# Two-layer trunk on one core: held modulation sums, solved rows on ScalarE, rope work kept out of the lead-in

## Chip, core and metric

One core of a Trainium2 chip runs the whole program. It has a matrix engine (TensorE, PE in the profile, with its weight loads as PEld), a vector engine (VectorE, DVE), a scalar engine (ScalarE, ACT), a general one (GpSimd, POOL) and an engine that issues the DMAs (SyncE, SP). Each engine takes its own instructions strictly in order; between engines they wait on semaphores. The metric is the device time of one launch in microseconds, the median of several runs.

## The reference

A decoder trunk of two layers on one sequence of 1024 tokens, 1024 wide, all in float32. Every layer norms its input, shifts and scales it with modulation vectors, projects it once, runs three token mixers on parts of the projection (causal pooling, retention with rotary positions, RWKV-7), gates and merges their outputs and adds the result back. Cut to what matters here:

```python
def rwkv7_time_mix(p, ...):
    ...
    def step(S, inp):
        r_t, w_t, k_t, v_t, a_t, b_t = inp
        sa = jnp.einsum('bhvk,bhk->bhv', S, a_t)
        S = (S * w_t[:, :, None, :] + sa[..., None] * b_t[:, :, None, :]
             + v_t[..., None] * k_t[:, :, None, :])
        return S, jnp.einsum('bhvk,bhk->bhv', S, r_t)
    _, y = lax.scan(step, jnp.zeros((B, H, N, N), jnp.float32), xs)
    ...

def rotary(x, positions):
    ang = positions.astype(jnp.float32)[..., None] * freqs
    cos, sin = jnp.cos(ang)[:, :, None, :], jnp.sin(ang)[:, :, None, :]
    ...

def hybrid_layer(x, c_act, positions, ...):
    mod = c_act @ w_ada + b_ada
    shift, scale, gate = jnp.split(mod[:, None, :], 3, axis=-1)
    h = rms_norm(x, norm_g) * (1.0 + scale) + shift
    proj = h @ w_in
    ...
    y = jnp.einsum('btnw,nwd->btnd', branches, w_branch)
    gates = jax.nn.sigmoid(gate_logits.reshape(B, T, N_BRANCHES, D))
    return x + gate * (jnp.sum(gates * y, axis=2) @ w_out)

def reference(x, c, positions, ...):
    c_act = jax.nn.silu(c)
    for l in range(2):
        x = hybrid_layer(x, c_act, positions, ...)
    return rms_norm(x, final_g)
```

## The kernel before

**Tiles.** The activations lie with channels on the 128 partitions and tokens in the free dimension, in two halves of 512 tokens; a 1024-wide tensor is 8 such tiles per half (kt 0 to 7). Float32 products are made of three passes: each operand is split into a rounded high part and the remainder (`hhi`/`hlo` for activations, `wh`/`wl` for weights), and high x high, low x high and high x low are summed in PSUM (`acc`). The high part is a cast, usually on ScalarE; the remainder is a subtraction on VectorE or GpSimd.

**The plan.** The Python program does not issue its instructions as it runs. From the lead-in on, each call is logged as an `Op` on one of five engines (`Log.call`, L217), so that all rows of the profile carry the helper's line, L540. `Log.plan` (L334) then lists them: at each point the engine that can start first takes the operation with the lowest key among those that are ready, by planned costs. The key is the place in the program plus a bias of the lane (`BIAS`): scan operations (lane rwkv) are put 3000 places ahead, modulation sums (lane ada) 1500 behind. Operations marked as free may go to VectorE or GpSimd, whichever the plan finds free. An entry `o.after[p] = 2` holds o until the planned start of p; it orders the plan and makes no semaphore. `emit` (L537) issues the result, and each engine keeps that order.

**Lead-in** (`lead_in`, L1810). The first three projections run while the norm and the modulation are still made. The modulation of layer 0 comes in groups: group g's weights are multiplied by the conditioning vector and added up on VectorE (`ada`, L696: eight rows, `ada_ps`, the last of them `ada_acc`), TensorE sums over the partitions (`sums`, one column each), and two small rows on VectorE make `mod` and `acoef` (`ada_end`, L736). With these ScalarE makes a tile's `hhi`, and a second activation makes the same value in full in place (`affine`, L1770); a subtraction (`low`, L1778) gives `hlo`; nine matmuls use both (`mms`, L1798). `coef(g)` is the whole of group g; groups 4 and 5 serve kt 4 to 7, and the call `coef(5)` ends the last of them. After the lead-in `setup_rest` (L661) loads and scales further vectors (`bone`, `vec`, `omu`), and `rope_tables` (L757) makes the sines and cosines for the two halves: `posi` and `ang`, some ten rows of range reduction on VectorE (`nrot`, `over`), two sines on ScalarE, and DMAs to DRAM (`rope_d`), from which `cs` tiles are read later.

**The scan** (`rwkv_task`, L1285). RWKV-7 runs as 16 chunks for each of 4 pairs of heads in each of 2 layers: 128 steps. In each, ScalarE scales the state (`SP`), TensorE multiplies the state (`two`), VectorE adds (`xst`), TensorE solves the chunk with a prepared inverse (`ch<-xst,G`), the solved rows are copied out of PSUM into `Z` (L1538), TensorE makes the state's update (`ch<-Z,BKt`), VectorE adds it to `S` (two rows), and TensorE makes the outputs (`two<-Z,G`), which ScalarE copies (`y`). Between these TensorE fills its time with the layer's large projections.

**Behind the scan** come the gate projections, merged by seven-product forms (sums of operands `T`, `wsum` on VectorE, then the same splitting), and the output projection. The other ten modulation groups, two of layer 0 and eight of layer 1 (`late_ada`, L1912), are queued in lane ada at this place of the program; a group is loaded in 256 KB tiles (`wada`), added up in `ada_acc` and summed by TensorE into `adaps`. They have no hold, so the plan starts them wherever VectorE has room, from inside layer 0's last scan on.

Of the kernel before, what the change touches and what calls it, by code (L numbers as in the profile page):

```python
# [12 lines left out]
AF = mybir.ActivationFunctionType  # L13
ALU = mybir.AluOpType
# [3 lines left out]
P = 128  # L18
# [186 lines left out]
class Log:  # L205


    def __init__(self, nc, tc):
        self.nc, self.tc = nc, tc
        self.on = False  # L210
        self.ops = []
        self.tag = {}
        self.acc = {}
        self.lane = ""
        self.group = None
        self.real = {"DVE": nc.vector, "POOL": nc.gpsimd}
        self.vector = Proxy(self, "DVE", nc.vector)  # L217
        self.scalar = Proxy(self, "ACT", nc.scalar)
        self.gpsimd = Proxy(self, "POOL", nc.gpsimd)
        self.tensor = Proxy(self, "PE", nc.tensor)  # L220
        self.sync = Proxy(self, "SP", nc.sync)

    def call(self, eng, name, real, a, k):
# [7 lines left out]
        if isinstance(o, Op):  # L231
            o.calls.append((real, a, k, name))
            o.outs += outs
            o.ins_ += ins
        else:
            o = Op()
            o.eng, o.calls, o.outs, o.ins_ = eng, [(real, a, k, name)], list(outs), list(ins)
            o.lane, o.n, o.late, o.inst = self.lane, name, not self.on, None
            o.no_dep = o.own_dep = o.behind = None
            o.held = False  # L240
            o.flex = self.on and FLEX and eng == "POOL" and name == "tensor_tensor" and self.lane in FREE and k.get("op") != ALU.pow
            o.after, o.allocs, o.took = {}, [], []
            o.idx = len(self.ops)
            self.ops.append(o)
            if self.on and self.group is not None:
                self.group = o
# [307 lines left out]
def trunk_kernel(ctx, tc, xT, cvec, pos, vecs, consts, w_ada, w_all, pool_w, lora_w, out):  # L554
# [374 lines left out]
    def add(k, task):  # L929
        if not lanes[k]:  # L930
            due[k] = clock[0]
        lanes[k].append(task)
        return task
# [351 lines left out]
    def rwkv_task(l, hp, kT, rT, vp, lt, lw):  # L1285
# [228 lines left out]
        for c in range(16):  # L1514
# [18 lines left out]
            for hd in range(2):  # L1533
# [1 line left out]
                u0 = (16 * hd + c) * P  # L1535
                n = min(65, 32 * P - u0 - 64)
                mmul(ch[0:n, cols], Gf[:, u0 + 64 : u0 + 64 + n], xst[:, cols])
            nc.vector.tensor_copy(Z[0:64, c, :], ch[0:64, 0:P])  # L1538
            yield wait(Z)
            mmul(ch[:, P : 2 * P], BKt[:, c, :], Z[:, c, :])  # L1540
            for hd in range(2):
# [228 lines left out]
    def affine(h, kt):  # L1770
        x = xin[h][kt]
        b, a = mod[0][:, SHIFT[kt] : SHIFT[kt] + 1], acoef[0][:, kt : kt + 1]
        hi, lo = hb("hhi"), hb("hlo")
        nc.scalar.activation(hi, x, AF.Identity, bias=b, scale=a)
        nc.scalar.activation(x, x, AF.Identity, bias=b, scale=a)
        h_cur[h].append((hi, lo))

    def low(eng, h, kt):  # L1778
# [27 lines left out]
    def steps(g, n):  # L1806
        for _ in range(n):
            next(g)

    def lead_in():  # L1810
        V, G_ = nc.vector, nc.gpsimd
# [30 lines left out]
        def coef(g):  # L1842
            if g in COLUMNS:
                ada_columns(g)
            else:
                steps(gs[g], 9)

        def one(h, kt):
            normed(h, kt)
            affine(h, kt)  # L1850
            low(G_, h, kt)
            mms(h, kt)
# [33 lines left out]
        one(1, 3)  # L1886
        one(0, 5)
        coef(5)
        one(1, 4)
        one(0, 6)  # L1890
        one(1, 5)
# [15 lines left out]
    for i in range(3):  # L1907
        evac(FIRST[i], acc6[1][i], 1)
    wprep()
    setup_rest()  # L1910
    add("mix", rope_tables())
    late_ada = [(0, g) for g in (6, 7)] + [(1, g) for g in range(8)]  # L1912

    for l in range(L):
# [46 lines left out]
                evac(it, ps, h)  # L1961
        assert not lanes["rwkv"] and not lanes["mix"]
        gate_ada = []
        add("ada", iter([30000]))
        while late_ada:
            task = add("ada", ada(*late_ada.pop(0), t_lt))
            if len(gate_ada) < 2:
                gate_ada.append(task)
        TT = [[] for _ in range(4)]
# [413 lines left out]
```

## Time and profile before

| | us |
|---|---|
| three runs | 2290.06, 2287.49, 2287.57 |
| median | 2287.57 |
| the profiled execution, its own time | 2284.81 |
| its span in the profile | 2282.9 |
| TensorE busy | 2246.9 |
| VectorE busy | 1627.5 |
| ScalarE busy | 907.4 |
| GpSimd busy | 623.8 |

The profiled execution's time is the span and 1.9 us around it. The mean granted clock of TensorE is 0.996. Matmuls overlap: one of 512 columns is shown with 0.39 us, but the next starts 0.227 us after it, so starts, not durations, tell the pace. "128x512 x6" stands for six like instructions in a run, and the number in brackets at a row's end is the idle time ahead of it, with the instruction that ended it. Stages in the trace: the lead-in up to about 115 us, layer 0's scan up to about 690, its gates and output up to about 1200, then layer 1.

### The profile page before, as it was taken

The numbers are of one execution on the slowest core, as the hardware profiler recorded it, in microseconds if no ns is written. First come the engines' busy times: TensorE is split into PE (matmuls) and PEld (weight loads), VectorE is DVE, ScalarE is ACT, GpSimd is POOL, SyncE is SP. The second block draws the span as 40 slices with busy tenths as digits, with TensorE's granted clock in tenths as the row PEclk, the third lists the DMA queues.
The fourth block names the chain that finished last, engine by engine and source line by source line (L and its number), as shares of the span: only waits on it lengthen the run. The fifth ranks groups of instructions, "written<-read, shape, count | busy, mean of one in ns | idle before, by whom it ended". The sixth has DMA issues, their size and how long they took to land.

```text
span 2282.9 us, 35125 instructions
## 1 busy us (share of the span) xinstructions
PE 2246.9 (98%) x13076; PEld 1866.6 (82%) x13076; DVE 1627.5 (71%) x2907; ACT 907.4 (40%) x1671; POOL 623.8 (27%) x545
## 2 busy tenths in 40 slices
PE   7999999999999999999999999999999999999998
PEld 6788888888888888888888888888888888888888
DVE  7997876878888644667677778688785844465854
ACT  5734433434235344323454344243332444442243
POOL 2223323323325201331122232332432500041211
PEclk9999999999999999999999999999999999999999
DMA  8212111112356633664541111111122633256442
GB/s 317 81 49 67 33 44 47 44 50 76 117 165 210 213 126 97 226 191 164 170 131 34 41 33 39 56 39 47 51 71 75 194 116 111 88 171 225 133 131 84
DMA packets 138043, 248.86 MB, mean 109 GB/s; under 512 B 15632, under 2 KB 18960, under 8 KB 137872
## 3 DMA queue, kind: packets, MB, share of 16 engines
q1 hardware_dynamic: 137872, 246.61, 33.9%
q8 instruction: 103, 1.69, 0.3%
q14 instruction: 68, 0.56, 0.1%
HBM read 187.04 MB, written 59.51 MB: 108 GB/s over the span
## 4 chain that ended last, share of the span: by engine, by line
PE 89%; DVE 8%; issue 1%; ACT 1%; DMA 0%; POOL 0%; SPq 0%; DVEq 0%; POOLq 0%; ACTq 0%
PE acc L540 73%; PE two L540 3%; PE ch L540 3%; PE av L540 1%; PE ro L540 1%; PE g L540 1%; DVE two L540 1%; DVE tm L540 1%; DVE ksq L540 1%; PE lw L540 1%; PE m L540 1%; PE rkv L540 1%; PE bt L540 1%; DVE G L540 1%; PE rs L540 0%
## 5 line engine op out<-in xcount | busy, mean ns | idle before, releaser
L540 PE MATMUL acc<-hhi,wh 128*128 128x512 f32 x1488 | 599.3, 403 | 0.6 <-DVE vp L540 0.6
L540 PE MATMUL acc<-hlo,wh 128*128 128x512 f32 x1488 | 598.5, 402 | 0.0
L540 PE MATMUL acc<-hhi,wl 128*128 128x512 f32 x1488 | 595.9, 401 | 0.0
L540 POOL TENSOR_TENSOR wl<-wr,wh 128x512 fp32r<-128x512 f32 x175 | 237.9, 1361 | 582.2 <-ACT wh L540 485.3
L540 PEld LDWEIGHTS acc<-hhi,wh 128*128 128x128 f32 x1488 | 280.6, 189 | 51.2 <-issue 1.5
L540 PEld LDWEIGHTS acc<-hhi,wl 128*128 128x128 f32 x1488 | 280.7, 189 | 49.2 <-issue 0.7
L540 PEld LDWEIGHTS acc<-hlo,wh 128*128 128x128 f32 x1488 | 280.8, 189 | 48.6 <-issue 0.7
L540 ACT CAST wh<-wr 128x512 fp32r<-128x512 f32 x242 | 149.1, 617 | 292.8 <-PE acc L540 230.0
L540 PE MATMUL acc<-T,wh 128*128 128x512 f32 x576 | 177.5, 390 | 0.0
L540 PEld LDWEIGHTS acc<-T,wh 128*128 128x128 f32 x576 | 108.2, 188 | 22.4
L540 DVE TENSOR_TENSOR wl<-wsum,wh 128x512 fp32r<-128x512 f32 x75 | 53.5, 713 | 94.8 <-ACT wh L540 94.4
L540 ACT COPY y<-two 64x128 f32<-64x128 f32 x128 | 32.9, 257 | 211.7 <-PE two L540 208.2
L540 PE MATMUL acc<-T,wl 128*128 128x512 f32 x288 | 112.3, 390 | 0.0
L540 DVE SCALAR_TENSOR_TENSOR S<-ch,pc,SP 64x64 f32<-64x64 f32 x256 | 71.9, 281 | 54.8 <-PE ch L540 46.8
L540 POOL TENSOR_TENSOR oz<-ol,oz 128x512 fp32r<-128x512 f32 x10 | 14.3, 1435 | 327.9 <-DVE wl L540 259.2
L540 ACT CAST wh<-wsum 128x512 fp32r<-128x512 f32 x96 | 59.5, 620 | 95.8 <-PE acc L540 93.7
L540 DVE TENSOR_TENSOR xst<-two,MT 64x128 f32<-64x128 f32 x128 | 37.5, 293 | 68.9 <-PE two L540 44.9
L540 DVE TENSOR_TENSOR two<-two,tm 64x30 f32<-64x30 f32 (+14 forms) x240 | 78.8, 328 | 7.0
L540 DVE TENSOR_TENSOR tm<-MT,two 64x30 f32<-64x30 f32 (+14 forms) x240 | 76.3, 318 | 8.2 <-ACT two L540 1.3
L540 DVE TENSOR_TENSOR wl<-wraw,wh 128x512 fp32r<-128x512 f32 x53 | 37.6, 710 | 61.5 <-ACT wh L540 61.5
L540 PE MATMUL acc<-oy,wh 128*128 128x512 f32 x256 | 80.0, 394 | 0.0
L540 PE MATMUL acc<-oG,wh 128*128 128x512 f32 x256 | 79.0, 390 | 0.0
(328 smaller groups left out, 4899.6 us busy)
## 6 DMA issues: line engine op xcount, KB each, us to landing
wr<-in_w_all SPq DMA_DIRECT2D x268, 256.0 KB, 2.7
wraw<-in_w_all SPq DMA_DIRECT2D x96, 256.0 KB, 2.7
gd<-gsg SPq DMA_DIRECT2D x96, 256.0 KB, 2.0
gs<-gd SPq DMA_DIRECT2D x96, 256.0 KB, 3.8
wada<-in_w_ada SPq DMA_DIRECT2D x80, 256.0 KB, 3.1
ol<-od SPq DMA_DIRECT2D x48, 256.0 KB, 3.4
traw<-hd SPq DMA_DIRECT2D x32, 256.0 KB, 3.0
x<-in_xT SPq DMA_DIRECT2D x16, 256.0 KB, 5.1
```

What stands on the lines that cost most here:

```text
L540: o.inst = f(*a, **k)
```

## The change

Four edits; the amount of work stays as it is.

1. `Z`, the copy of the solved rows, goes from VectorE to ScalarE (128 rows).
2. In `affine` the second activation goes to VectorE for kt 6 and 7 (four rows).
3. What `setup_rest` and `rope_tables` put on VectorE, ScalarE and GpSimd is not planned ahead of the start of `coef(5)`'s last operation. Their DMAs have no hold.
4. What the ten late modulation groups put on these three engines is not planned ahead of the start of the last scan operation of layer 0. Their DMAs and matmuls have no hold of their own.

```diff
@@ Log.call
+            if self.quiet is not None and eng in ("DVE", "ACT", "POOL"):
+                o.after[self.quiet] = 2
@@ rwkv_task
-            nc.vector.tensor_copy(Z[0:64, c, :], ch[0:64, 0:P])
+            nc.scalar.copy(Z[0:64, c, :], ch[0:64, 0:P])
@@ affine
-        nc.scalar.activation(x, x, AF.Identity, bias=b, scale=a)
+        if kt < 6:
+            nc.scalar.activation(x, x, AF.Identity, bias=b, scale=a)
+        else:
+            nc.vector.tensor_scalar(x, x, a, b, op0=ALU.mult, op1=ALU.add)
@@ 
+    coefs = []
+
+    def quietly(gen, until_=None):
+        while True:
+            nc.quiet = until_ or coefs[0]
+            dt = next(gen, None)
+            nc.quiet = None
+            if dt is None:
+                return
+            yield dt
@@ lead_in
         coef(5)
+        coefs.append(nc.ops[-1])
@@ 
+    nc.quiet = coefs[0]
     setup_rest()
-    add("mix", rope_tables())
+    nc.quiet = None
+    add("mix", quietly(rope_tables()))
@@ for l in range(L)
+        last_ = next(o for o in reversed(nc.ops) if o.lane == "rwkv")
...
-            task = add("ada", ada(*late_ada.pop(0), t_lt))
+            task = add("ada", quietly(ada(*late_ada.pop(0), t_lt), last_))
```

The plan moves other rows too. Three places, each as it was and as it is now (the helper's line is L543 in the changed kernel).

VectorE in the lead-in, around the sums of group 4 (`ada_acc_204`) and the start of group 5 (`ada_ps_213`); before:

```order
L540 TENSOR_SCALAR vec_101<-vec_101 128x28
L540 SCALAR_TENSOR_TENSOR ada_ps_205<-ringG_130,fixed,ada_ps_205 128x512
L540 TENSOR_SCALAR vec_101<-vec_101 128x4 x2
L540 SCALAR_TENSOR_TENSOR ada_ps_205<-ringG_130,fixed,ada_ps_205 128x512 x2
L540 SCALAR_TENSOR_TENSOR ada_acc_204<-ringG_130,fixed,ada_ps_205 128x512
L540 CAST ang_280<-posi_279 128x512
L540 TENSOR_SCALAR ada_ps_213<-wada_189,fixed 128x512
L540 TENSOR_TENSOR wl_230<-wr_231,wh_229 128x512
L540 SCALAR_TENSOR_TENSOR ada_ps_213<-wada_189,fixed,ada_ps_213 128x512
L540 TENSOR_TENSOR mod_108<-sums_157,vec_100 128x4
L540 SCALAR_TENSOR_TENSOR ada_ps_213<-wada_189,fixed,ada_ps_213 128x512
L540 SCALAR_TENSOR_TENSOR acoef_110<-mod_108,vec_100 128x2
```

and in the changed kernel:

```order
L543 TENSOR_TENSOR wbig_139<-wr_188,wbig_139 128x512
L543 SCALAR_TENSOR_TENSOR ada_ps_205<-ringG_130,fixed,ada_ps_205 128x512 x5
L543 SCALAR_TENSOR_TENSOR ada_acc_204<-ringG_130,fixed,ada_ps_205 128x512
L543 TENSOR_SCALAR ada_ps_213<-wada_189,fixed 128x512
L543 SCALAR_TENSOR_TENSOR ada_ps_213<-wada_189,fixed,ada_ps_213 128x512 x2
L543 TENSOR_TENSOR mod_108<-sums_157,vec_100 128x4
L543 SCALAR_TENSOR_TENSOR acoef_110<-mod_108,vec_100 128x2
L543 SCALAR_TENSOR_TENSOR ada_ps_213<-wada_189,fixed,ada_ps_213 128x512
L543 SCALAR_TENSOR_TENSOR ada_ps_213<-wada_190,fixed,ada_ps_213 128x512
```

The rows of `vec`, `ang` and the weight remainder `wl_230` are gone from this stretch (`bone` and `omu`, a little ahead of it, as well), and `mod` and `acoef` follow each other behind three rows of group 5; before, two of these stood ahead of `mod` and one behind it. The remainders `wl_230` and `wbig_137` are made on GpSimd now.

ScalarE at the sines of the second half, early in the first scan (`y` ends one step, `SP` begins the next); before:

```order
L540 ACT_TABLE_LOAD
L540 ACTIVATE nrot_294<-nrot_294 64x512
L540 ACTIVATE nrot_294<-ang_293 64x512
L540 COPY y_417<-two 64x128
L540 CAST wh_384<-wr_386 128x512
L540 COPY pu_408<-acc_402 128x512
L540 ACTIVATE SP_424<-S_406,pc_270 128x128
L540 CAST pw_436<-pwraw_438 128x128
L540 COPY y_417<-two 64x128
L540 ACTIVATE SP_441<-S_405,pc_270 128x128
L540 CAST pdh_446<-pd_444 128x512
L540 CAST wh_387<-wr_389 128x512
```

and in the changed kernel:

```order
L543 ACTIVATE SP_443<-S_406,pc_270 128x128
L543 ACT_TABLE_LOAD
L543 ACTIVATE nrot_294<-nrot_294 64x512
L543 COPY Z_269<-ch_445 64x128
L543 ACTIVATE nrot_294<-ang_293 64x512
L543 CAST pdh_446<-pd_444 128x512
L543 COPY y_417<-two 64x128
L543 ACTIVATE SP_448<-S_405,pc_270 128x128
L543 ACT_TABLE_LOAD
L543 ACTIVATE silu_428<-acc_416 128x512
L543 CAST wh_395<-wr_397 128x512
L543 COPY Z_269<-ch_449 64x128
```

`Z` stands between `SP` and `y` in every step. The second half's sines (`nrot_294`) have moved three steps on, and both `Z` here have a table load between their step's `SP` and them.

VectorE at the end of layer 0's last scan (`xst`, `Z` and `S` are the scan's, `T` and `traw` belong to the forms behind it); before:

```order
L540 TENSOR_TENSOR traw_1285<-traw_1285,traw_1286 128x512
L540 COPY Z_1032<-ch_1264 64x128
L540 SCALAR_TENSOR_TENSOR rob_1243<-rot_1242,vec_100,silu_1179 128x512
L540 SCALAR_TENSOR_TENSOR ada_acc_1460<-wada_1477,fixed,ada_acc_1460 128x256
L540 SCALAR_TENSOR_TENSOR S_1195<-ch_1264,pc_1033,SP_1263 64x64 x2
L540 SCALAR_TENSOR_TENSOR ada_acc_1460<-wada_1477,fixed,ada_acc_1460 128x256
L540 TENSOR_SCALAR ada_acc_1497<-wada_1498,fixed 128x256
L540 TENSOR_TENSOR xst<-two,MT_1117 64x128
L540 SCALAR_TENSOR_TENSOR ada_acc_1497<-wada_1498,fixed,ada_acc_1497 128x256
L540 SCALAR_TENSOR_TENSOR ada_acc_1497<-wada_1499,fixed,ada_acc_1497 128x256
L540 TENSOR_TENSOR mod_109<-adaps_1496,vec_101 128x2
L540 COPY Z_1032<-ch_1266 64x128
```

and in the changed kernel:

```order
L543 TENSOR_TENSOR traw_1286<-traw_1286,traw_1283 128x512
L543 SCALAR_TENSOR_TENSOR S_1195<-ch_1264,pc_1029,SP_1263 64x64 x2
L543 TENSOR_TENSOR yc_1234<-yc_1234,vr_1236 128x512
L543 TENSOR_TENSOR xst<-two,MT_1117 64x128
L543 TENSOR_TENSOR traw_1285<-traw_1285,traw_1286 128x512
L543 SCALAR_TENSOR_TENSOR rob_1249<-rot_1248,vec_100,silu_1179 128x512
L543 TENSOR_TENSOR wl_1169<-wr_1170,wh_1168 128x512
L543 SCALAR_TENSOR_TENSOR S_1194<-ch_1266,pc_1029,SP_1265 64x64 x2
L543 TENSOR_REDUCE mn_1267<-y_1246 128x8
L543 TENSOR_SCALAR mn_1267<-mn_1267 128x8
L543 TENSOR_TENSOR T_1302<-traw_1275,T_1302 128x512
L543 TENSOR_TENSOR T_1303<-traw_1283,T_1303 128x512
```

The modulation rows (`ada_acc`, `mod`) that lay between the scan's rows are gone from here, and the rows of `Z` with them.

More of the change, by code (lines that the diff above doesn't have):

```diff
@@ L215, in __init__ @@
         self.group = None
+        self.quiet = None
         self.real = {"DVE": nc.vector, "POOL": nc.gpsimd}
```

## The prediction

> **What bounds the kernel now.** I read the page first (busy time, then the chain of waits), after it the list of what TensorE waited for, and then the timeline at the places of the three edits.
>
> ```profile
> PE 2246.9 (98%) x13076; PEld 1866.6 (82%) x13076; DVE 1627.5 (71%) x2907; ACT 907.4 (40%) x1671; POOL 623.8 (27%) x545
> PE 89%; DVE 8%; issue 1%; ACT 1%; DMA 0%; POOL 0%; SPq 0%; DVEq 0%; POOLq 0%; ACTq 0%
> ```
>
> TensorE is busy for 2246.9 of 2282.9 us, and the chain that ended last runs through it. The change leaves all its matmuls in place, so only the 36 us in which it stands idle, and matmuls that ran slower than others of their kind, can be won. VectorE at 71% and ScalarE at 40% matter where TensorE waits for them:
>
> ```profile
> PE sums L540 <- DVE sq L540: 6.8, 2, 6.1
> PE acc L540 <- ACT hhi L540: 3.1, 3, 2.2
> PE ch L540 <- DVE Z L540: 2.7, 4, 1.2
> PE acc L540 <- DVE hlo L540: 0.9, 1, 0.9
> PE adaps L540 <- DVE ada_acc L540: 0.7, 2, 0.5
> PE acc L540 <- DVE vp L540: 0.6, 1, 0.6
> ```
>
> The columns are us in total, times, and the longest. The largest wait, for sq, lies at the program's start, which no edit touches. The waits for hhi, hlo and vp belong to the lead-in, those for Z to the scan, those for ada_acc to the modulation sums: these the edits can reach, some 8 us in all.
>
> **The lead-in.** TensorE sums modulation group 4, then stands still until the first operand that needs the result is there:
>
> ```profile
> 52.83 0.95 PE L540 MATMUL sums<-fixed,ada_acc 128*128 128x1 f32 x8
> 56.01 2.92 PE L540 MATMUL acc<-hhi,wbig 128*128 128x512 f32 x6 [2.23 <-ACT hhi L540]
> 58.73 1.00 PE L540 MATMUL acc<-hlo,wbig 128*128 128x512 f32 x3
> ...
> 47.63 0.68 DVE L540 TENSOR_SCALAR vec<-vec 128x28 f32<-128x28 f32 x1
> 51.10 0.75 DVE L540 SCALAR_TENSOR_TENSOR ada_acc<-ringG,fixed,ada_ps 128x512 f32<-128x512 f32 x1
> 51.77 0.42 DVE L540 CAST ang<-posi 128x512 f32<-128x512 int32 x1
> 52.89 0.69 DVE L540 TENSOR_TENSOR wl<-wr,wh 128x512 fp32r<-128x512 f32 x1
> 54.16 0.15 DVE L540 TENSOR_TENSOR mod<-sums,vec 128x4 f32<-128x4 f32 x1
> 54.95 0.15 DVE L540 SCALAR_TENSOR_TENSOR acoef<-mod,vec 128x2 f32<-128x2 f32 x1
> 55.14 0.81 ACT L540 ACTIVATE hhi<-x,mod,acoef 128x512 fp32r<-128x512 f32 x1 [2.28 <-DVE acoef L540]
> ```
>
> The sums end at 53.78 (52.83 + 0.95). mod starts at 54.16 because VectorE is still at a piece of group 5, and another such piece stands between mod and acoef (54.95 - 54.16 = 0.79 between their starts, though mod takes 0.15). VectorE got behind by work that nobody needs yet: the vector scaling, the rope cast, one weight remainder. In the new order these rows stand behind group 5's coefficients, mod and acoef stand side by side, and three pieces of group 5 are done before the sums end. So mod starts at about 53.8, acoef 0.13 later, hhi 0.19 behind that (55.14 - 54.95): at 54.14 instead of 55.14. I take 0.95 us, and TensorE's gap shrinks from 2.23 to about 1.3. Less than nothing can't come of it, since ScalarE had 2.28 us idle ahead of hhi; the other bound is 0, if the weight remainder that goes to GpSimd in this order, or a row that I don't see, is late in VectorE's stead.
>
> The length of the gap matters twice:
>
> ```profile
> 56.00:58.00 2.00, 1.99 (x5) 1.61 (x6) 1.97 (x4) 1.97 (x3) 0.00 (x0) 0.50 0.17 67
> 59.00:60.00 1.00, 1.00 (x5) 0.81 (x5) 0.96 (x3) 1.00 (x3) 0.72 (x1) 0.97 0.68 262
> 1131.00:1135.00 4.00, 2.28 (x11) 1.50 (x10) 3.90 (x7) 2.08 (x4) 3.51 (x2) 1.00 0.54 205
> ...
> 29.82 1.44 PE L540 MATMUL sums<-fixed,sq 128*128 128x1 f32 x6 [2.04 <-DVE mod L540]
> 30.00:34.00 4.00, 4.00 (x14) 3.52 (x15) 3.28 (x7) 1.76 (x3) 1.28 (x1) 0.50 1.07 390
> ...
> 1133.93 0.50 PE L540 MATMUL acc<-mhi,wl 128*128 128x512 f32 x1 [1.72 <-POOL wl L540]
> ...
> 817.56 293.05 PE acc L540 x1288
> ```
>
> The third number from the right is the granted clock. It is 0.50 behind the gap of 2.23 us and behind an earlier one of 2.04, but 1.00 around a gap of 1.72. The nine matmuls behind the longer gap take from 56.01 to 59.73 (58.73 + 1.00), 3.7 us. The last row, of the chain of waits, has the pace at full clock: 293.05 / 1288 = 0.227 us each, so nine are 2.0. The clock costs 1.7 at most; I take 1.5, as the end of the last matmul overlaps with its successor. A gap of 1.3 lies below the 1.72 that cost nothing, so I count the 1.5 as won, with 0 as the other bound.
>
> [...]
>
> Two more stalls in the lead-in go with the edit of the x affine and the rope rows:
>
> ```profile
> 74.08 1.28 ACT L540 ACT_TABLE_LOAD   x1
> 75.38 0.63 ACT L540 ACTIVATE lt<-lt 64x512 f32<-64x512 f32 x1
> 75.92 0.80 ACT L540 ACTIVATE x<-x,mod,acoef 128x512 f32<-128x512 f32 x1
> 76.75 0.69 DVE L540 TENSOR_TENSOR hlo<-x,hhi 128x512 fp32r<-128x512 f32 x1 [1.35 <-ACT x L540]
> 77.49 0.50 PE L540 MATMUL acc<-hlo,wbig 128*128 128x512 f32 x1 [0.95 <-DVE hlo L540]
> ```
>
> The last x sits on ScalarE behind a table load; VectorE waits for it 1.35 us and TensorE 0.95 (1.1 with the pipeline's refill). With x on VectorE the pair x, hlo needs two rows of about 0.7 there and doesn't wait for ScalarE; in the new order it stands right behind the small vector work (some 1.9 us), far ahead of 77. That is 1.1 won. The wait for vp (0.6) was behind rope rows on VectorE; those are now later than the second evacuation, so I count it as won, 0 as the bound. The four x rows cost VectorE 4 x 0.7 = 2.8 us in a stretch in which it loses the rows above; if that cover fails, one hlo is late by 0.7. The rope's results come later with them: in the new order the second half's sine falls three scan steps later, and its first reader on VectorE stands four steps behind it, so I let nothing wait. Lead-in: 0.95 + 1.5 + 1.1 + 0.6 = 4.2 us won, bounds 1.7 (only the last two) and 4.5.
>
> **Z on ScalarE.** The scan has 128 steps, each with one Z. An ordinary step, the one bad step, and the copy's price on the new engine:
>
> ```profile
> 360.13 0.28 DVE L540 COPY Z<-ch 64x128 f32<-64x128 f32 x1 [0.76 <-PE ch L540]
> 360.91 0.38 PE L540 MATMUL ch<-Z,BKt 128*128 128x128 f32 x2
> ...
> 1721.44 1.75 DVE L540 SCALAR_TENSOR_TENSOR pd<-pt,pu 128x512 f32<-128x512 f32 x1 [0.82 <-POOL pt L540]
> 1723.22 0.28 DVE L540 COPY Z<-ch 64x128 f32<-64x128 f32 x1
> 1723.55 0.49 PE L540 MATMUL ch<-Z,BKt 128*128 128x128 f32 x2 [1.19 <-DVE Z L540]
> ...
> L540 ACT COPY y<-two 64x128 f32<-64x128 f32 x128 | 32.9, 257 | 211.7 <-PE two L540 208.2
> L540 ACT CAST wh<-wr 128x512 fp32r<-128x512 f32 x242 | 149.1, 617 | 292.8 <-PE acc L540 230.0
> ```
>
> In the ordinary step Z is done at 360.41 and used at 360.91: 0.5 us to spare. A copy of that shape out of PSUM takes 257 ns on ScalarE (the y row) against 280, so the copy itself is worth nothing. What counts is the queue ahead of it. On VectorE that was once a row of 1.75 us, twice modulation rows of the last scan; these waits, 2.7 in all, are the whole gain, and I take 2.4. On ScalarE I counted in the new order what stands between a step's SP and its Z: nothing in 46 steps, one of 512 columns (or small ones) in 57, two in 13, and more in four; the remaining eight are first steps, whose SP comes early. SP is done some 1.4 us before Z can start, so one or two rows of 0.6 fit. Of the four, two have a table load (1.28) ahead of Z: 1.28 + 0.6 to 1.28 + 1.2 is late by 0.5 to 1.1 once 1.4 is taken off, and two of 1.8 and 2.4 by 0.4 to 1.0, each less the 0.5 to spare. I take 1.0 lost, bounds 0 and 2.5. VectorE has 128 x 0.28 = 36 us less to do, which shows nowhere else, since TensorE waits for it at no other place of the scan for over 0.7.
>
> [...] In this trace the next activation starts 0.02 us behind the load (74.08 + 1.28 = 75.36, then 75.38). [...]
>
> **The held sums.** The first answer is that of the modulation rows alone in the last scan, the others are all engines behind it:
>
> ```profile
> 500.00:690.00 190.00, 3.19 (x24) 3.27 (x24) 23.46 (x35) 1.00 0.38 116
> ...
> 690.00:725.00 35.00, 35.00 (x157) 28.96 (x157) 29.77 (x36) 18.89 (x35) 23.82 (x17) 1.00 0.68 220
> 725.00:760.00 35.00, 35.00 (x159) 29.04 (x159) 26.42 (x40) 14.20 (x25) 10.39 (x8) 1.00 0.60 195
> ```
>
> 23.46 us of VectorE in 35 rows move behind the scan's end at about 690, with 24 one-column matmuls (the DMAs aren't held, so their queue keeps its order nearly). VectorE has 5.2 and 8.6 us free in the two stretches there, TensorE none: what the sums push back there, TensorE feels. But the sums rank lowest in the plan, and in the new order only one of their rows stands among the first 25 behind the scan, ahead of which all first operands of the forms are made. Nothing reads them before the layer's end. The price is that of their own matmuls' waits: 0.7 in two waits for six groups before, so 0.6 more for four more groups; bounds 0 and 9.7 (23.46 less 13.8 free), the latter as a rival.
>
> **Sum.** -4.2 - 2.4 + 1.0 + 0.6 = -5.0 us. The profiled execution took 2284.81 us for a span of 2282.9, so it would be 2279.8; it stands 2.8 below the median of the runs, 2287.57, and the runs are what counts: 2282.6. A plan that is drawn up anew shifts other rows too; from the size of the small waits above (0.6 to 1.7 each) I allow 3 us either way.
>
> **Rivals.**
>
> 1. The clock halves again behind the shorter gap. For it: 2.04 us were enough, and nothing says where between 1.72 and 2.04 it turns, or that length alone decides. The 1.5 is gone: 2284.1.
>
> 2. The gap in the lead-in stays, since something else is late (the weight remainder on GpSimd, the sums themselves): the edit doesn't do what it says. Against it: 2.28 us of ScalarE's idle time end with acoef. 0.95 + 1.5 are gone and one of the small stalls returns: 2286.
>
> 3. Z is late on ScalarE, and the kernel is slower. Place: every step in which a 617 ns cast starts just before Z can. To spare are 0.5 us in good steps and less in others, and a cast that in turn waits for TensorE (230 of the 292.8 us idle ahead of casts ended with acc) drags Z along, as a copy has to wait for what is ahead in its queue. Such a step loses about 0.3. It decides from 5 / 0.3, some 17 steps, on. If it strikes the half of the steps with a row ahead, 64 x 0.3 = 19 us are lost, less what is won: about 2297 for some 50. Against it: the plan keeps Z ahead of casts (46 steps with nothing), and ScalarE is busy only 40% of the time.
>
> 4. The held sums crowd VectorE behind the scan: 9.7 us of operands late in 690 to 760, 2282.6 - 0.6 + 9.7 = 2291.7. It decides when sums stand ahead of the forms' operands; the order speaks against it.
>
> 5. The new plan packs better elsewhere with 36 us less on VectorE: 3 us more, 2279.6.
>
> **How the numbers follow.** Forecast 0.48 (its own range 2279.5 to 2285.5), rival 1 0.14, rival 2 0.08, rival 3 0.14, rival 4 0.08, rival 5 0.08. A measurement of this kernel tells about 0.2% (4.6 us) from no change, so faster is below 2283.0 and slower above 2292.1. Faster: three quarters of the forecast, 0.36, all of rival 5, a little of rival 1: 0.46. Slower: nearly all of rival 3, half of rival 4: 0.18. Same: 0.36. The range for 8 in 10 goes from 2277, where the upper bounds of the gains and the better plan lie, to 2292, which takes in rivals 1, 2 and most of 4, and leaves out rival 3.
>
> **What would show it.** In the profile after: TensorE's wait for hhi at about 55 is near 1.3 and the clock of the next 2 us is 1.00 (step one right; 0.50 is rival 1); no wait for hlo at 75 and none for vp near 93; the line "ch <- Z" names ACT with about 1 us in two to five waits (20 or more waits are rival 3); in 690 to 760 TensorE stays fully busy (if not, rival 4). The prediction is wrong if TensorE's idle time is not about 5 us less, or if the idle time is less and the span isn't, as matmuls then ran slower than I take them to.

## The result, and the profile after

The changed kernel takes 2278.0 us (median of 5 runs, 2277.56 to 2279.91) against 2287.57 (5 runs, 2285.1 to 2290.06): a ratio of 0.9960 with a 95% interval of 0.9948 to 0.9971, so 6.6 to 11.9 us less. The forecast was 5.0 us less. The profiled execution is the median one, 2278.0, and its span 2275.7 us, 7.2 shorter than the span before; the medians differ by 9.6, since the profiled execution before was 2.8 below its median. TensorE's idle time in the spans went from 36.0 to 28.5 us.

What TensorE waited for in the changed kernel, in the list that the prediction began with (us in total, times, longest):

```profile
PE acc L543 <- ACT hhi L543: 1.8, 2, 1.3
PE acc L543 <- POOL wl L543: 1.7, 1, 1.7
PE two L543 <- DVE S L543: 1.2, 4, 0.4
PE nps L543 <- ACT sg L543: 1.2, 2, 0.8
PE adaps L543 <- DVE ada_acc L543: 0.5, 1, 0.5
PE ch L543 <- ACT Z L543: 0.2, 1, 0.2
```

The waits for hlo and vp are gone, the longest for hhi is at 1.3 instead of 2.2, that for Z at 0.2 instead of 2.7. New are small waits for S and for sg. The lead-in, TensorE first, then VectorE and ScalarE:

```profile
52.83 0.95 PE L543 MATMUL sums<-fixed,ada_acc 128*128 128x1 f32 x8
55.07 2.19 PE L543 MATMUL acc<-hhi,wbig 128*128 128x512 f32 x6 [1.30 <-ACT hhi L543]
57.06 1.49 PE L543 MATMUL acc<-hlo,wbig 128*128 128x512 f32 x3
58.34 1.81 PE L543 MATMUL acc<-hhi,wbig 128*128 128x512 f32 x5
...
53.81 0.16 DVE L543 TENSOR_TENSOR mod<-sums,vec 128x4 f32<-128x4 f32 x1
54.01 0.16 DVE L543 SCALAR_TENSOR_TENSOR acoef<-mod,vec 128x2 f32<-128x2 f32 x1
...
54.20 0.81 ACT L543 ACTIVATE hhi<-x,mod,acoef 128x512 fp32r<-128x512 f32 x1 [3.24 <-DVE acoef L543]
```

The sums end where they ended before, at 53.78. mod follows at 53.81, acoef at 54.01, hhi at 54.20, and TensorE stands still for 1.30 us: as worked out. But look at the rows behind the gap: nine matmuls from 55.07 to 58.34 take 3.27 us, where nine at full clock, 0.227 us each, take 2.0. In the windows of the same profile (the third number from the right is the granted clock):

```profile
54.00:56.00 2.00, 0.93 (x4) 0.80 (x5) 1.69 (x4) 1.76 (x3) 0.00 (x0) 0.99 0.22 85
56.00:58.00 2.00, 2.00 (x7) 1.51 (x6) 1.81 (x3) 1.97 (x3) 0.00 (x0) 0.50 0.35 131
58.00:60.00 2.00, 2.00 (x8) 1.59 (x7) 1.55 (x3) 2.00 (x4) 0.39 (x1) 0.65 0.34 131
```

The clock is whole until 56 and halved then, a little later than before. So the first rival came true at this place, and yet the kernel gained more than the forecast. The rest must come from the scans.

**A wait that the list doesn't show.** Here is a step of layer 1's scan before, VectorE and then TensorE. The list of waits has no wait for Z in this step, since no row carries a bracket:

```profile
1459.92 0.68 DVE L540 TENSOR_TENSOR rot<-acc,cs 64x512 f32<-64x512 f32 x1
1460.64 0.28 DVE L540 COPY Z<-ch 64x128 f32<-64x128 f32 x1
...
1459.41 0.40 PE L540 MATMUL ch<-xst,G 128*65 128x64 f32 x4
...
1460.52 0.47 PE L540 MATMUL acc<-hhi,wh 128*128 128x512 f32 x1
1460.98 0.49 PE L540 MATMUL ch<-Z,BKt 128*128 128x128 f32 x2
```

The solved product is done at 1459.81. VectorE began a row of rot at 1459.92, and Z had to wait until 1460.64. It ended at 1460.92, and TensorE's product of it started 0.06 behind. The matmul ahead had started at 1460.52, so the next could have begun 0.23 later, at 1460.75: 0.23 us were lost. The list calls TensorE idle only from the shown end of a matmul, 0.47 behind its start, and so misses some 0.2 us of each wait of this kind. By starts, a step is late when `ch<-Z` begins within 0.08 us of Z's end, and what it loses is the distance from the matmul ahead beyond 0.23. Before, that is 10 steps with 2.9 us in layer 0 and 8 with 2.4 in layer 1: 5.3 us where the list had 2.7 in four waits. In all 18, Z stands directly behind a row of VectorE (rot seven times, also ksq, ka, wl, traw and others, of 0.16 to 1.75 us). So it does in 68 of the other 110 steps too; the 18 have in common that Z starts 0.69 us or more behind the solved product, where the median of the others is 0.04. In the changed kernel one step of the 128 is late, by 0.4 us.

### The profile page after: what moved, and what is told of

Its sections match the earlier page's. It is cut to its first block, busy times and chain, and to the rows that moved or that the text cites. A ratio compares the mean times of both kernels' runs of the same rounds, so it can differ in the third digit from the quotient of the medians.

```text
span 2275.7 us, 35073 instructions
## 1 busy us (share of the span) xinstructions
PE 2247.2 (99%) x13076; PEld 1868.3 (82%) x13076; DVE 1613.4 (71%) x2779; ACT 934.2 (41%) x1795; POOL 626.1 (28%) x549
## 4 chain that ended last, share of the span: by engine, by line
PE 90%; DVE 6%; issue 1%; ACT 1%; DMA 1%; POOL 0%; SPq 0%; DVEq 0%; POOLq 0%; ACTq 0%
PE acc L543 74%; PE two L543 3%; PE ch L543 2%; PE g L543 1%; PE av L543 1%; PE ro L543 1%; DVE ksq L543 1%; PE m L543 1%; PE bt L543 1%; PE lw L543 1%; PE rkv L543 1%; PE rs L543 1%; DVE G L543 0%; PE pps L543 0%; DVE two L543 0%
## 5 line engine op out<-in xcount | busy, mean ns | idle before, releaser
L543 PE MATMUL acc<-hhi,wh 128*128 128x512 f32 x1488 | 597.9, 402 | 0.0
L543 PE MATMUL acc<-hhi,wl 128*128 128x512 f32 x1488 | 596.9, 401 | 0.0
L543 PE MATMUL acc<-hlo,wh 128*128 128x512 f32 x1488 | 596.3, 401 | 0.0
L543 POOL TENSOR_TENSOR wl<-wr,wh 128x512 fp32r<-128x512 f32 x164 | 222.6, 1359 | 563.0 <-ACT wh L543 402.5
L543 PEld LDWEIGHTS acc<-hhi,wh 128*128 128x128 f32 x1488 | 280.5, 189 | 49.8 <-issue 1.8
L543 PEld LDWEIGHTS acc<-hhi,wl 128*128 128x128 f32 x1488 | 280.4, 188 | 49.6 <-issue 0.7
L543 PEld LDWEIGHTS acc<-hlo,wh 128*128 128x128 f32 x1488 | 280.5, 189 | 49.4 <-issue 1.1
L543 ACT CAST wh<-wr 128x512 fp32r<-128x512 f32 x242 | 149.1, 617 | 264.7 <-PE acc L543 202.6
L543 PE MATMUL acc<-T,wh 128*128 128x512 f32 x576 | 178.1, 390 | 0.0
L543 DVE SCALAR_TENSOR_TENSOR S<-ch,pc,SP 64x64 f32<-64x64 f32 x256 | 72.2, 282 | 87.0 <-PE ch L543 83.9
L543 PEld LDWEIGHTS acc<-T,wh 128*128 128x128 f32 x576 | 108.0, 188 | 22.3
L543 PE MATMUL acc<-T,wl 128*128 128x512 f32 x288 | 112.4, 390 | 0.0
L543 DVE TENSOR_TENSOR wl<-wsum,wh 128x512 fp32r<-128x512 f32 x69 | 49.2, 713 | 81.6 <-ACT wh L543 81.2
L543 ACT CAST wh<-wsum 128x512 fp32r<-128x512 f32 x96 | 59.5, 620 | 94.8 <-PE acc L543 92.9
L543 POOL TENSOR_TENSOR oz<-ol,oz 128x512 fp32r<-128x512 f32 x10 | 14.0, 1401 | 281.6 <-DVE wl L543 212.7
L543 DVE TENSOR_TENSOR xst<-two,MT 64x128 f32<-64x128 f32 x128 | 37.5, 293 | 68.3 <-PE two L543 47.7
L543 DVE TENSOR_TENSOR two<-two,tm 64x30 f32<-64x30 f32 (+14 forms) x240 | 78.9, 329 | 7.3
L543 ACT COPY Z<-ch 64x128 f32<-64x128 f32 x128 | 33.0, 258 | 123.3 <-PE ch L543 123.1
L543 DVE TENSOR_TENSOR tm<-MT,two 64x30 f32<-64x30 f32 (+14 forms) x240 | 76.3, 318 | 10.2 <-ACT two L543 3.4
L543 PE MATMUL acc<-oy,wh 128*128 128x512 f32 x256 | 80.2, 394 | 0.0
L543 PE MATMUL acc<-oG,wh 128*128 128x512 f32 x256 | 79.0, 390 | 0.0
L543 PE MATMUL acc<-oz,wh 128*128 128x512 f32 x256 | 78.9, 389 | 0.0
```

What stands on the lines that cost most here:

```text
L543: o.inst = f(*a, **k)
```

## The experiments

Each further kernel was timed in five rounds beside the kernel before on the same chip. Late steps are counted in the profiled execution, as above. The changed kernel itself was timed apart from them, so a difference between a median here and its 2278.0 is uncertain by some 3 to 4 us, as the intervals of both ratios add to it.

| kernel | median us | ratio to before, 95% interval | late steps (us lost), layer 0 | layer 1 |
|---|---|---|---|---|
| before | 2287.2 to 2288.4 | 1 | 10 (2.9) | 8 (2.4) |
| changed | 2278.0 | 0.9960 [0.9948, 0.9971] | 1 (0.4) | 0 |
| z_only | 2280.1 | 0.9967 [0.9955, 0.9980] | 2 (0.1) | 0 |
| z_undone | 2285.5 | 0.9989 [0.9980, 0.9998] | 11 (2.4) | 8 (2.3) |
| hold_undone | 2277.41 | 0.9952 [0.9940, 0.9965] | 2 (0.3) | 0 |
| quiet_undone | 2280.89 | 0.9967 [0.9954, 0.9979] | 1 (1.4) | 0 |
| x_undone | 2278.47 | 0.9963 [0.9951, 0.9976] | 2 (1.0) | 0 |
| two_edits | 2280.6 | 0.9970 [0.9959, 0.9981] | 3 (1.0) | 0 |
| z_layer1 | 2284.61 | 0.9988 [0.9979, 0.9997] | 9 (2.3) | 1 (0.2) |
| before_reserve | 2291.65 | 1.0023 [1.0014, 1.0032] | 8 (2.4) | 9 (1.4) |
| crowd | 2289.43 | 1.0011 [1.0003, 1.0020] | 2 (2.3) | 4 (0.4) |
| fill | 2278.02 | 0.9961 [0.9947, 0.9974] | 2 (0.4) | 0 |
| before_shake | 2290.17 | 1.0014 [1.0005, 1.0023] | 8 (2.3) | 8 (0.7) |
| after_shake | 2278.94 | 0.9961 [0.9948, 0.9973] | 2 (1.4) | 0 |

One execution also differs from another by where it stands before any edit acts: before and z_only issue the same rows in the same order up to 168 us, and z_only is 0.9 us later all the same. The traces allow for this. Each has 7792 matmuls of 512 columns; this is how much later than in the changed kernel the nth of them starts, in us (in brackets its time there):

| kernel | 40th (45) | 400th (148) | 3000th (926) | 7700th (2194) |
|---|---|---|---|---|
| before | 0.0 | 1.83 | 4.22 | 7.15 |
| z_only | 0.87 | 2.74 | 2.61 | 2.75 |
| z_undone | -0.60 | -0.59 | 3.89 | 7.12 |
| z_layer1 | 1.05 | 3.26 | 8.17 | 8.77 |
| hold_undone | 0.01 | -0.01 | 0.14 | 0.25 |
| quiet_undone | 1.12 | 2.47 | 3.46 | 3.62 |
| x_undone | 0.57 | 1.62 | 0.72 | 0.76 |

What a kernel loses between two columns is the difference of its numbers. The 40th lies ahead of the first wait that an edit changes, the 400th in front of the first scan, the 3000th in the work behind layer 0's scan.

The theories were these. A: VectorE's queue held the scan's products back, and Z is the edit that matters. B: the edits only redraw the plan, and any redraw moves the time by as much. C: the gain comes from the held sums and the lead-in, and Z is worth its listed waits at most.

**z_only**, the kernel before with one line changed:

```diff
-            nc.vector.tensor_copy(Z[0:64, c, :], ch[0:64, 0:P])
+            nc.scalar.copy(Z[0:64, c, :], ch[0:64, 0:P])
```

> The kernel before with one edit of the four: the solved rows Z copied on ScalarE. The changed kernel's span is 7.2 us shorter than before, and by segments of the trace about 2.6 of it lie in layer 0's scan and 3.5 in layer 1's. Theory A (VectorE's queue was what held the scan's products back, and Z is the edit that shortens it): both scans gain alone, some 5 to 6 us, about 2282, and TensorE's wait for Z is nearly gone. Theory B (the four edits only redraw the plan, and any redraw moves small waits by some 3 us): within 3 us of before. Theory C (the gain in the scans is the held sums' and the lead-in's): at most the 2.7 us of TensorE's waits for Z, about 2285, and nothing more in layer 1 than the 1.2 us of its one wait.

It was 2280.1, 4.6 to 10.3 us below before by its interval: A's 5 to 6 lie inside, C's 2.7 outside. Of the 18 late steps two are left. In the traces, before loses 7.2 us from the 40th matmul to the 7700th and z_only 1.9, so Z is worth 5.3 between these two executions, as much as the late steps lost (5.3 less 0.1). The other 1.9 are there by the 400th matmul: they are the lead-in's, and they are kept to the end.

**z_undone**, the changed kernel with the same line reversed.

> The changed kernel with Z back on VectorE, the other three edits kept. Theory A: 5 to 6 us of the 9 are lost, about 2283.5, and layer 1's scan (which no other edit touches directly) is as long as before. Theory B: within 3 us of the changed kernel. Theory C: 1 to 2.7 us lost, about 2280.

It was 2285.5, 7.5 above the changed kernel (6.6 by the ratios): some three quarters of the gain, as A says. From the 3000th matmul on, behind layer 0's scan, it loses 3.2 us and before 2.9: layer 1 is as slow as before, as A says too. The late steps are back, and the list of waits has its row of before again:

```profile
PE ch L543 <- DVE Z L543: 2.1, 3, 1.2
PE bon L543 <- DVE G L543: 0.7, 1, 0.7
PE rs L543 <- DVE wob L543: 0.6, 1, 0.6
```

The rows for bon and rs are those of the kernel before to the tenth, and the changed kernel lacks the first and has 0.2 in the second: with Z in VectorE's queue, other rows there are late too. In the traces z_undone loses 7.7 us from the 40th matmul on, 3.4 more than its late steps explain (4.7 less 0.4). These other waits are where I look for the rest; it wasn't tried apart, and between before and z_only no such rest is left.

**z_layer1**, the kernel before with Z on ScalarE in layer 1 alone:

```diff
-            nc.vector.tensor_copy(Z[0:64, c, :], ch[0:64, 0:P])
+            (nc.scalar.copy if l else nc.vector.tensor_copy)(Z[0:64, c, :], ch[0:64, 0:P])
```

> The kernel before with Z on ScalarE in layer 1 only. If each late Z costs what the starts of TensorE's matmuls show (18 steps and 5.3 us in both layers, 8 steps and 2.4 us in layer 1), layer 1's scan gains 2.4 to 3.5 us and layer 0's plan is the old one with its ten late steps: about 2285. If a gain needs Z on ScalarE throughout, or is a matter of the redrawn plan, layer 0's late steps change too.

It was 2284.61, 2.6 below before, with nine late steps left in layer 0 and one in layer 1. From the 3000th matmul to the 7700th it loses 0.6 us where before loses 2.9, so 2.3 are won there, as the late steps say (2.4 less 0.2). The gain falls where the edit is. Layer 0 was slower in this execution than before although TensorE, VectorE and ScalarE have the same rows in the same order up to 1281 us: the clock was halved for 6.8 us at 620 (last section).

**before_shake and after_shake**, the two kernels under one and the same random disturbance of the plan:

```diff
-SEED = 0
-SHAKE = 0
+SEED = 1
+SHAKE = 40
```

> The kernel before under another plan: the rows' order is disturbed by up to 20 places at random (scan rows excepted), nothing else. It shows how much a redrawn plan alone moves the time. Theory A, in which the gain is that of the edits: before under this plan may stand anywhere within some 4 us of 2287.5, but the pair of this run and the next keeps a difference of 6 us or more. Theory B: the scatter is as large as the 9 us, and the pair differs by less than 4.

> The changed kernel under the same disturbance. Theory A: 6 us or more below the kernel before under it, with at most two or three steps in which Z has under 0.08 us to spare, against 12 or more there. Theory B: less than 4 us below it.

Before moved to 2290.17 (interval 1.1 to 5.3 us above), the changed kernel to 2278.94. The pair differs by 11.2 us, and the late steps are 16 against 2. B falls: a redraw is worth some 3 us, as the prediction allowed, and the four edits together are worth more than that under either plan (two plans were tried). Part of this pair's difference is the clock: in before_shake's profile it is halved for 6.8 us from 54 on and for 3.4 from 624 on, in after_shake's only for 3.4 from 57 on.

**hold_undone**, the changed kernel without the hold on the modulation sums:

```diff
-            task = add("ada", quietly(ada(*late_ada.pop(0), t_lt), last_))
+            task = add("ada", ada(*late_ada.pop(0), t_lt))
```

> The changed kernel without the hold on the late modulation sums. Theory A: the sums return to the last scan of layer 0 but no Z stands behind them on VectorE any more, so little is lost there, and the 1 us that TensorE idles more behind the scan comes back: within 1.5 us of the changed kernel. Theory C: 2 to 4 us lost, about 2281.

It was 2277.41, the lowest median of all, though its interval covers the changed kernel. This edit brought nothing that could be measured once Z was off VectorE. C falls here too. In the changed kernel the held sums found room behind the scan (windows; the third pair in a row is VectorE):

```profile
690.00:725.00 35.00, 34.94 (x156) 28.45 (x155) 30.18 (x31) 14.95 (x27) 22.72 (x15) 1.00 0.69 225
725.00:760.00 35.00, 35.00 (x164) 29.19 (x163) 27.71 (x38) 13.87 (x24) 12.19 (x9) 1.00 0.64 211
760.00:800.00 40.00, 40.00 (x185) 33.23 (x184) 29.22 (x53) 16.08 (x28) 10.61 (x9) 1.00 0.62 195
800.00:860.00 60.00, 59.55 (x275) 49.34 (x274) 43.77 (x58) 24.13 (x42) 17.32 (x14) 1.00 0.65 211
```

TensorE stays busy, and VectorE has taken the sums over the whole stretch; behind 800 they are 23.17 us of its work, against 5.98 before, when it was busy there for 30.64 us:

```profile
800.00:860.00 60.00, 60.00 (x270) 49.76 (x269) 30.64 (x49) 25.22 (x44) 5.59 (x4) 1.00 0.40 128
```

The stretch has 43.77 now.

**quiet_undone**, the changed kernel without the hold on vectors and rope work:

```diff
-    nc.quiet = coefs[0]
     setup_rest()
-    nc.quiet = None
-    add("mix", quietly(rope_tables()))
+    add("mix", rope_tables())
```

> The changed kernel without the hold on the vectors and the rope work (Z, the x affine and the held sums kept). If the lead-in's gain of about 2.9 us up to the first scan is kept to the end: 2 to 3 us lost, about 2280.5, with TensorE's wait for hhi near 2.2 us again. If the scan gives it back anyway: no loss, 2278.

It was 2280.89, 2.9 above the changed kernel (1.6 by the ratios), and its gap ahead of hhi is back at 2.1 us. In the traces it loses 2.5 us from the 40th matmul on: 1.4 by the 400th, and 1.0 of what follows is one late Z (1.4 us, against 0.4 in the changed kernel), which in this kernel stands on ScalarE behind a table load and two sines. So the lead-in's gain is kept to the end, and it is 1.4 to 1.9 us, not 4.2.

**x_undone**, the changed kernel with `affine` as it was, **and two_edits**, with the hold on the sums undone as well, so that Z and the hold on vectors and rope work remain:

```diff
-        if kt < 6:
-            nc.scalar.activation(x, x, AF.Identity, bias=b, scale=a)
-        else:
-            nc.vector.tensor_scalar(x, x, a, b, op0=ALU.mult, op1=ALU.add)
+        nc.scalar.activation(x, x, AF.Identity, bias=b, scale=a)
```

> The changed kernel with the second x activation of kt 6 and 7 back on ScalarE. If the stall for hlo (1.1 us between starts before) was ended by this edit, it is back and 1 us is lost: 2279. If it was ended by the work that left VectorE, nothing is lost: 2278.

> Only Z on ScalarE and the hold on vectors and rope work; neither the x affine nor the hold on the modulation sums. Each of these two alone was worth less than 1 us when undone, so together: within 1.5 us of the changed kernel, 2278 or a little less. If one stood in for the other, 2 to 3 us more.

x_undone was 2278.47, no measurable loss, and its list has no wait for hlo. The stall that the prediction put down to the x affine was ended by the work that left VectorE. The trace does lose 1.0 us between the 40th and the 400th matmul, where it has two new waits for other rows of ScalarE (lw at 82, pu at 94), but by the 3000th that is made up. two_edits was 2280.6, 2.6 above the changed kernel, so my expectation missed: the two edits stand in for each other to some degree, or the plan of this kernel fell 2 us worse (it has three late steps with 1.0 us). With a scatter of 3 us between plans, these runs don't settle which.

**before_reserve**, the kernel before, whose plan keeps an engine free for an urgent row a little sooner:

```diff
-                soon = [h for h in c if h.lane in HOT and h.key < o.key and t < h.ready < t + 0.7 * o.occ]
+                soon = [h for h in c if h.lane in HOT and h.key < o.key and t < h.ready < t + 1.0 * o.occ]
```

> The kernel before (Z on VectorE) with one number of the plan changed: an engine is kept free for an urgent row that becomes ready within 1.0 of the time that another row would take, where it was 0.7. If Z was late because VectorE was in the middle of a row of 0.7 us or more when the solved product arrived, the 18 steps in which TensorE took Z with less than 0.08 us to spare (5.3 us lost in them by the starts of its matmuls) become fewer, under 10, and the time falls by 1 to 4 us below before. If the engine itself mattered (its way to PSUM, or the copy), the number stays near 18 and the time within 2 us of before.

It was 2291.65, 4 us above before, with 17 late steps. Neither expectation holds: the steps did not become fewer, and the time left the 2 us around before. The rule works on every engine but TensorE, and in the lead-in alone the wait for hhi grew to 3.4 us. By the 150th matmul of 512 columns (75 us) this kernel has lost 6.1 us more than before, so its loss arose there:

```profile
PE acc L540 <- ACT hhi L540: 3.7, 2, 3.4
PE two L540 <- DVE S L540: 2.7, 4, 1.8
```

In each of the 17, Z again stands directly behind a row that VectorE had begun. The run says that this number of the plan doesn't mend it; whether Z could be had in time on VectorE by another plan stays open.

**crowd**, the changed kernel with five more copies of the small row ahead of Z on ScalarE:

```diff
             nc.scalar.activation(SP, S, AF.Copy, scale=pcc)
+            for _ in range(5):
+                nc.scalar.activation(SP, S, AF.Copy, scale=pcc)
```

> The changed kernel with five more copies of the small row SP in each of the 128 scan steps, ahead of Z on ScalarE: some 5 x 0.31 = 1.5 us more in ScalarE's queue per step, 200 us in all, with the same result. If room in the queue ahead of Z is what the change bought, Z is late again in many steps: 10 or more with under 0.08 us to spare, and 3 us or more of the gain lost, 2281 or above. If ScalarE has room for it (it is done with SP some 1.4 us before Z can start, and TensorE has 0.5 us to spare), little is lost: under 2 us.

It was 2289.43, 11.4 above the changed kernel and slower than before: with some 1.5 us more in ScalarE's queue per step (an estimate: five rows at 0.31, the distance from an SP at 203.46 to the next row at 203.77 in the changed kernel) nothing of the gain is left. But only six steps are late, by 2.7 us, fewer than I expected. So the run shows that ScalarE must have room, not that Z is what suffers first; most of the loss lies elsewhere. Some of the waits stand here beside that for Z, and the clock was halved for 3.4 us from 704 on:

```profile
PE ch L543 <- ACT Z L543: 2.1, 1, 2.1
PE rkt L543 <- DVE rsm L543: 2.0, 2, 1.8
PE acc L543 <- ACT wh L543: 1.8, 2, 1.4
```

**fill**, hold_undone with work for TensorE in the gap of the lead-in; the six products are written beside the sums and read by nobody:

```diff
         steps(gs[4], 9)
+        for _ in range(6):
+            mmul(sums_ps[0][0][:, 256:512], wparts[0][0][0][:, 3 * P : 4 * P], h_cur[0][3][0][:, 0:256])
```

> The changed kernel without the hold on the modulation sums, and with six matmuls of 256 columns whose result nobody reads, put behind group 4's sums where TensorE stands idle for 1.30 us in the lead-in. In the traces so far the clock was halved after stretches of 2.08 us and more without a 512-column matmul (group 4's one-column sums counted as idle) and stayed whole after 1.96 and less. If so, the clock stays at 1.00 behind this gap, the eight matmuls that ran at 0.427 us run at 0.23, and the time is about 1.4 us below the same kernel without the fill: 2276. If the clock follows something else, such as windows of its own, it is halved as before and the time is 2277.4 or more.

Windows, and TensorE's rows:

```profile
54.00:56.00 2.00, 1.75 (x15) 1.55 (x13) 1.89 (x6) 0.70 (x1) 0.00 (x0) 1.00 0.47 131
56.00:58.00 2.00, 1.93 (x8) 1.30 (x8) 1.73 (x3) 1.93 (x4) 0.00 (x0) 1.00 0.09 35
58.00:60.00 2.00, 2.00 (x10) 1.62 (x10) 1.77 (x4) 2.00 (x4) 0.00 (x0) 1.00 0.57 216
...
53.92 0.95 PE L543 MATMUL sums<-fixed,ada_acc 128*128 128x1 f32 x8
55.12 0.97 PE L543 MATMUL sums<-hhi,wbig 128*128 128x256 f32 x6 [0.26 <-DVE mod L543]
56.17 1.66 PE L543 MATMUL acc<-hhi,wbig 128*128 128x512 f32 x6
57.74 0.97 PE L543 MATMUL acc<-hlo,wbig 128*128 128x512 f32 x3
58.55 1.31 PE L543 MATMUL acc<-hhi,wbig 128*128 128x512 f32 x5
...
66.32 1.91 PE L543 MATMUL acc<-hhi,wbig 128*128 128x512 f32 x7 [0.53 <-ACT hhi L543]
```

The clock stays at 1.00, and from the sums to the end of the nine matmuls it takes 4.63 us (53.92 to 58.55) instead of 5.51 in the changed kernel (52.83 to 58.34): 0.9 us won, though the fill waits 0.26 for mod and delays the first matmul. In the changed kernel the matmuls behind these nine are slow too, so by its 100th matmul of 512 columns (64 us) fill has won 1.4, as expected. By the 150th (75 us) 0.9 of it is lost again: TensorE got ahead of ScalarE and waits 0.53 for the next hhi. The median, 2278.02 against 2277.41 without it, shows none of this; so small an effect is below what these medians tell apart.

## Why the prediction was right, and where it was not

**The lead-in's first step held to 0.06 us.** Forecast were mod at 53.8, hhi at 54.14 and a gap of about 1.3; it is 53.81, 54.20 and 1.30.

**The clock did not.** The term of 1.5 us rested on a gap of 1.72 that cost nothing. Rival 1 was right: the clock halved behind 1.30 as well. The nine matmuls took 3.56 us before (56.01 to 59.57) and 3.27 now, but the half clock lasts as long as before and now falls on work in full, where before its first 0.4 us fell into the gap (the kernel before, then the changed one):

```profile
55.64:59.05 3.41, 3.04 (x7) 2.47 (x8) 3.38 (x6) 3.34 (x6) 0.62 (x1) 0.50 0.23 85
55.98:59.39 3.41, 3.41 (x10) 2.65 (x9) 3.18 (x5) 3.38 (x5) 0.00 (x0) 0.50 0.40 154
```

At half the clock 3.04 us of work lose 1.5 and 3.41 lose 1.7, so 0.2 were lost here where 1.5 were to be won. By the 100th matmul of 512 columns (64 us) the changed kernel is 0.7 us ahead: the gap's 0.9 less these 0.2. The step that failed is the comparison of gaps; the length of the gap in the list did not decide (see the last section).

**hlo and vp** are gone as forecast, 1.7 us, but the stall of hlo went for another reason than I gave (x_undone), and a new wait of 0.77 us for sg came at 79.74, in the same stretch. In sum the lead-in won 1.8 to 1.9 us by the 400th matmul (before and z_only, in the table of matmuls), where 4.2 were forecast.

**Z was mis-sized.** The forecast has 2.4 won and 1.0 lost to ScalarE's queue, 1.4 net. Measured are 5.3 between the profiled executions of before and z_only, and more between medians (7.5 for z_undone, 6.6 by the ratios). Two errors add up. The gain was read off the list of waits, 2.7 us in four steps; by the starts of the matmuls it is 5.3 in 18. And the loss to ScalarE's queue, table loads and all, is 0.4 in one step. This is it, ScalarE first, then TensorE:

```profile
195.48 1.28 ACT L543 ACT_TABLE_LOAD   x1
196.77 0.60 ACT L543 ACTIVATE silu<-acc 128x512 f32<-128x512 f32 x1
197.26 0.61 ACT L543 CAST wh<-wr 128x512 fp32r<-128x512 f32 x1
197.78 0.26 ACT L543 COPY Z<-ch 64x128 f32<-64x128 f32 x1
...
198.09 0.49 PE L543 MATMUL ch<-Z,BKt 128*128 128x128 f32 x2 [0.20 <-ACT Z L543]
```

The load is followed by the next activation at once (195.48 + 1.28 = 196.76, then 196.77), as in the row of before that the prediction shows: 0.01 us lie between them here, 0.02 there. The other step with a load, at 193.21, was in time.

**Rival 3**, Z late on ScalarE, did not occur, for the reason given against it; crowd shows how much room it took: some 1.5 us more per step and the kernel is slower than before.

**The held sums** were to cost 0.6; they cost nothing that can be measured, and they bring nothing either (hold_undone). Rival 4 is excluded by the windows above.

So the time came out in the range and on the forecast side, 4.6 us below the forecast, and partly by luck: the lead-in won 1.9 instead of 4.2, Z 5.3 instead of 1.4, and the held sums cost 0 instead of 0.6. Two terms were wrong by more than 2 us each, in opposite directions, and the range up to 2292 was wide enough to hold the kernel before as well. The 1.9 and 5.3 add up to the 7.2 by which the spans differ. TensorE's idle time, by which the prediction wanted to be judged, fell by 7.5 us and not by about 5; the span did follow it. The 2.4 by which the medians differ more were not traced; one candidate is the clock in executions of before that weren't profiled (last section).

## What to carry to other kernels

Where an engine runs overlapping instructions back to back, read its waits from the distance between starts: a list of idle times shows only what exceeds the overlap, and here it showed half (2.7 of 5.3 us). Two single executions are compared from a point ahead of the edit, at equal work done; here that took up to 1.1 us of scatter out. A small copy in the middle of a recurrence belongs on the engine whose queue is shortest when its input arrives, even if the copy is hardly faster there (here 260 ns on ScalarE against 282 on VectorE, medians of 128, and 5.3 us won). Before a hold or a reorder is credited, undo it alone: two of the four edits here, each undone by itself, cost nothing that could be measured.

## What the runs showed of the hardware

Whether the clock was halved behind a thin stretch of TensorE work was not settled by the stretch's length alone. In the lead-in, 2.08 us without a 512-column matmul (group 4's sums and the 1.30 gap) halved it in seven kernels, while in z_layer1 2.06 us that ended at 38.47 did not, nor did this gap of the changed kernel, with a granted clock of 1.00 in the windows 1126 to 1130 and 1130 to 1134:

```profile
1130.09 0.50 PE L543 MATMUL acc<-mhi,wl 128*128 128x512 f32 x1 [1.71 <-POOL wl L543]
```

Clearer is a pair of executions of the same work. Up to 1281 us before and z_layer1 have the same rows in the same order on TensorE, VectorE and ScalarE. In the last scan of layer 0 the clock was halved in z_layer1 and not in before (before, then z_layer1 with its windows):

```profile
619.15 0.56 PE L540 MATMUL adaps<-fixed,ada_acc 128*128 128x1 f32 x4
619.57 0.48 PE L540 MATMUL acc<-hhi,wl 128*128 128x512 f32 x1
...
620.76 0.96 PE L540 MATMUL adaps<-fixed,ada_acc 128*128 128x1 f32 x4
621.59 0.78 PE L540 MATMUL acc<-hhi,wl 128*128 128x512 f32 x1
616.99:620.40 3.41, 2.99 (x44) 2.42 (x43) 2.41 (x4) 1.19 (x3) 1.27 (x1) 1.00 0.02 5
620.40:627.22 6.82, 6.82 (x28) 5.87 (x29) 2.51 (x8) 1.20 (x3) 0.55 (x1) 0.50 0.38 115
```

Ahead of it TensorE was busy for 2.99 of 3.41 us, but with many small matmuls: of 32 x 32, and one-column sums. By the 3000th matmul z_layer1 lost 2.9 us more than before for it. before_shake (3.4 us from 624 on) and before_reserve (3.4 from 629 on) show it behind the same rows. These are three of the four kernels that have both the sums and Z on VectorE in that scan; in the profiles of the other ten the clock is whole there. Whether it strikes executions of before that weren't profiled no trace shows; their times spread over 5 us, those of the changed kernel over 2.4.

In the 14 profiles every half-rate stretch but those at the start and at the end lasted 3.41 us or twice that, and in the lead-in it came at different distances from the restart: 0.4 us ahead of it in before, 0.3 behind it in z_undone, 0.9 in the changed kernel (eight matmuls of 0.427 in z_undone, at 54.83 to 58.24). In before two of these stretches, at 28.38 to 35.21 and at 55.64 to 59.05, lie 20.43 us apart, which is six times 3.41 (20.46). From these lengths and distances I estimate that the clock is set for pieces of 3.41 us that don't begin anew when TensorE restarts; what decides whether a piece is halved no run shows. fill, with 0.26 us of idle time at this place, kept the clock whole (1.00 from 52 to 62).
